# Split weights at rotating offsets inside their slots, in a one-layer decoder kernel

## The chip, the core and the metric

The kernel runs on one core of a Trainium2 chip. A core has a matrix engine, TensorE (PE in the profile; its weight loads have a row of their own, PEld), a vector engine (DVE), an engine for activation functions (ACT), a general one (POOL) and a queue that mostly issues transfers (SP). All but the last work on a memory of 128 partitions on the core; in this text a "column" is one 4-byte element of each partition. Matmul results go to a separate accumulation memory of eight banks. The metric is the device time of one execution in microseconds; lower is better. The time before is 1580.56 us, the median of three runs that went from 1579.78 to 1582.54 us.

## The reference

One layer of a hybrid decoder computes 256 prompt tokens and 8 single-token samples, 264 token columns in all, with a model width of 2048:

```
xn = rmsnorm(x, g_mix);  z = xn @ w_in
x  = x + concat(rglru_group(z), mlstm_group(z)) @ w_out
xq = rmsnorm(x, g_xa) @ w_xa_q
x  = x + cross_attention(xq, memory K/V) @ w_xa_o      # 4 heads of 512, 256 memory tokens
xf = rmsnorm(x, g_ffn)
x  = x + (silu(xf @ w_ffn_gate) * (xf @ w_ffn_up)) @ w_ffn_down   # inner width 5632
y  = rmsnorm(x, g_final)
```

For the prompt, the memory's keys and values are also projected from 256 memory tokens (`mem @ w_xa_k`, `mem @ w_xa_v`); for the samples they come from a cache. States of the recurrent groups, keys and values are outputs as well. All is 32-bit floating point, and nearly all of the arithmetic is in the products with the weights.

## The kernel before

Activations lie transposed: the model width on the partitions, tokens along the columns. A product with weights is cut into steps (the list `steps`); a step has one weight piece of 128 partitions by up to 2048 columns (1 MB), which yields 128 output rows for all 264 tokens. `load_piece` (line 142) brings piece i into one of three `raw` buffers from the SP queue, some steps ahead.

To keep 32-bit accuracy with fast matmuls, each operand is held as a high and a low part of a reduced-precision 32-bit type. `split_half` (line 150) does that for the weights, 1024 columns at a time: ACT writes the high part `wh`, a rounded copy of the raw piece, and DVE writes the low part `wl`, the raw piece minus `wh`. Each goes to one of four slots of its own (tags "wh" and "wl"), in turn. The activations are split in the same way by other helpers into tiles of tag "B", of which there are 26 slots; one such tile usually holds four chunks of 264 columns.

`mm3` (line 175) then multiplies with three matmuls per chunk of 128 columns of weights:

```
pe.matmul(ps, ah, bh, start=start, stop=False)
pe.matmul(ps, ah, bl, start=False, stop=False)
pe.matmul(ps, al, bh, start=False, stop=stop)
```

The first argument after `ps` is the operand that is loaded into the array, the second the one that streams. In the normal steps (`proj`), the loaded operand is a chunk of `wh`, `wh` again, then `wl`, and the streamed ones are chunk c of the activation's high part, of its low part, and of its high part again. A full step has 16 chunks and 48 matmuls. In the value projection (`pe_v`) the roles are swapped: the activation is loaded and 512 columns of `wh` or `wl` stream. The matmuls of the key projection stream 256 columns, those of the other steps 264.

The main loop at the end goes through the steps in order. It issues the load of a later piece, the evaluation of the step before's result, the splits of the next step's piece (`split_half(i + LS, 0)` and `(…, 1)`, at high priority), the step's matmuls, and then as much side work (gates, recurrences, attention for the samples on DVE and ACT) as an estimate of the engines' clocks allows. The order on each engine is settled by a scheduler that simulates the program's timeline; only SP's order is written out by hand.

The profile puts almost all instructions on line 60, the helper that records them, so its rows are told apart by tiles: `mm<-B,wh` is a matmul into an accumulation bank `mm`, streaming a B tile against a high part.

Of the kernel before, what the change touches and what calls it, by code (L numbers as in the profile page):

```python
# [11 lines left out]
F32R = mybir.dt.float32r  # L12
# [5 lines left out]
P = 128  # L18
# [62 lines left out]
def layer_kernel(ctx: ExitStack, tc, xT, memT, vec, wrg, w_in, w_out, w_q, w_k, w_v, w_o,  # L81
# [7 lines left out]
    sb = ctx.enter_context(tc.tile_pool(name="sb", bufs=1))  # L89
# [6 lines left out]
    def nm(s):  # L96
        uid[0] += 1
        return f"{s}_{uid[0]}"
# [51 lines left out]
    def split_half(i, h, parts=1):  # L150
        if i >= len(steps):
            return
        cols = steps[i][1]
        lo, hi = h * 1024, min(cols, (h + 1) * 1024)
        wh = sb.tile([P, 1024], F32R, tag="wh", bufs=4, name=nm("wh"))
        wl = sb.tile([P, 1024], F32R, tag="wl", bufs=4, name=nm("wl"))
        r = raws[i]
        n = (hi - lo) // parts
        with tc.high_priority():
            for o in range(0, hi - lo, n):  # L160
                st["split"] = act.activation(wh[:, o: o + n], r[:, lo + o: lo + o + n], AF.Copy)
                dve.tensor_sub(wl[:, o: o + n], r[:, lo + o: lo + o + n], wh[:, o: o + n])
        splits[i, h] = (wh, wl)
# [1027 lines left out]
    with tc.high_priority():  # L1191
        for c in range(KC):
            split(*xn(c), xres[:, c, :], V("g_mix", c))
            if c == 1:
                split_half(0, 0, 4)
            elif c == 3:
                split_half(0, 1, 2)

    pend = []
    for i, (src, cols, pef, evf, need) in enumerate(steps):  # L1200
# [12 lines left out]
        now = pe.clock  # L1213
        dve.clock, act.clock = max(dve.clock, now), max(act.clock, now)
        split_half(i + LS, 0)
        if i + LS < len(steps) and steps[i + LS][1] > 1024:
            split_half(i + LS, 1)
# [128 lines left out]
```

## Time and profile before

| | |
|---|---|
| median of three runs | 1580.56 us |
| the profiled execution's span, first to last instruction | 1577.6 us |
| TensorE matmuls, busy | 1560.9 us (99%), 12,356 |
| TensorE weight loads, busy | 1536.0 us (97%), 12,356 |
| DVE, busy | 1047.3 us (66%) |
| ACT, busy | 779.2 us (49%) |
| mean granted TensorE clock | 0.994 of full speed |
| from HBM to the core and back | 205 GB/s over the span |

A row of the groups reads: line, engine, operation, output from inputs, shape, count, then busy time in us, the mean duration of one in ns, and the idle time of the engine just before them with what ended it. Matmuls overlap in the pipeline, so the duration of one (285 ns) is far longer than the interval between two starts. In the table by stretches, a cell such as "100.00 (x827)" is the engine's busy time in the stretch and the number of its instructions that start there; PEclk is the granted clock, 1.00 being full speed. In the order of time, a row gives the start and the length in us of a run of like instructions and, after "x", how many there are.

### The profile page before, as it was taken

Reading aid. Unit: us, or ns where it says so; the run is one execution under the profiler, and the core shown is the slowest. Engines: PE = TensorE matmul, PEld = TensorE weight load, DVE = VectorE, ACT = ScalarE, POOL = GpSimd, SP = SyncE. Lnnn points to the kernel's source line nnn. Section 1 sums busy time; section 2 is a strip of 40 time slices with the busy share of each in tenths; the row PEclk is TensorE's granted clock in tenths of the full one; section 3 lists DMA queues with packets and bytes.
Section 4 is the critical chain, followed back from the end, with each engine's and each line's share of the span. In section 5 each row is a group of like instructions: output and inputs, shape, how many; then the busy total and the mean of one; then the engine's idle time right before and its main releaser. Section 6 shows DMA issues by size and latency. Waiting matters only on the chain.

```text
span 1577.6 us, 29752 instructions
## 1 busy us (share of the span) xinstructions
PE 1560.9 (99%) x12356; PEld 1536.0 (97%) x12356; DVE 1047.3 (66%) x2019; ACT 779.2 (49%) x1217; POOL 74.9 (5%) x142
## 2 busy tenths in 40 slices
PE   9999999999999999999999999999999999999997
PEld 9999999999999889989999999999999999999997
DVE  7976878787689999856655555455555554555554
ACT  7465775564445555545444444333444433344463
POOL 0001210001012112000000000000000000000000
PEclk9999999999999999999999999999999999999999
DMA  8445875547689888554545555455445555555452
GB/s 311 154 174 171 303 262 202 189 159 260 247 298 353 314 330 302 178 182 180 187 163 185 188 181 173 182 187 186 174 178 185 188 181 174 180 188 188 153 180 97
DMA packets 55303, 325.97 MB, mean 207 GB/s; under 512 B 6688, under 2 KB 7120, under 8 KB 24448
## 3 DMA queue, kind: packets, MB, share of 16 engines
q1 hardware_dynamic: 39744, 270.68, 47.9%
q0 software_dynamic: 15136, 53.16, 9.2%
q8 instruction: 96, 1.57, 0.4%
q10 hardware_dynamic: 288, 0.23, 0.1%
q14 instruction: 39, 0.32, 0.1%
HBM read 312.78 MB, written 11.28 MB: 205 GB/s over the span
## 4 chain that ended last, share of the span: by engine, by line
PE 97%; ACT 1%; DVE 1%; DMA 0%; issue 0%; SPq 0%; DVEq 0%; ACTq 0%
PE mm L60 92%; PE ax L60 6%; DVE B L60 1%; ACT B L60 1%; DMA xres<-xT 0%; ACT wh L60 0%; ACT L60 0%; DVE wl L60 0%; DVE c L60 0%; DVEq L1323 0%; DVE xres L60 0%; ACT t L60 0%; SPq L1185 0%; ACT rstd L60 0%; SPq L1178 0%
## 5 line engine op out<-in xcount | busy, mean ns | idle before, releaser
L60 PE MATMUL mm<-B,wh 128*128 128x264 f32 (+1 forms) x7520 | 1380.0, 285 | 2.8 <-DVE B L60 2.8
L60 PEld LDWEIGHTS mm<-B,wh 128*128 128x128 f32 x7520 | 1166.8, 189 | 4.4 <-ACT cso L60 2.9
L60 PE MATMUL mm<-B,wl 128*128 128x264 f32 (+1 forms) x3760 | 1066.9, 284 | 1.2 <-DVE wl L60 1.2
L60 ACT ACTIVATE wh<-raw 128x1024 fp32r<-128x1024 f32 (+2 forms) x518 | 538.4, 1041 | 710.1 <-PE mm L60 584.1
L60 DVE TENSOR_TENSOR wl<-raw,wh 128x1024 fp32r<-128x1024 f32 (+2 forms) x518 | 620.7, 1200 | 370.0 <-ACT wh L60 361.8
L60 PEld LDWEIGHTS mm<-B,wl 128*128 128x128 f32 x3760 | 708.8, 189 | 1.6 <-DVE wl L60 1.4
L60 DVE TENSOR_TENSOR t<-mm,rstd 128x264 f32<-128x264 f32 x104 | 44.9, 432 | 57.5 <-PE mm L60 57.5
L60 PE MATMUL mm<-wh,B 128*128 128x512 f32 x256 | 83.0, 398 | 0.0
L60 DVE TENSOR_TENSOR xres<-xres,mm 128x264 f32<-128x264 f32 x80 | 34.3, 428 | 46.5 <-PE mm L60 46.5
L60 PEld LDWEIGHTS mm<-wh,B 128*128 128x128 f32 x256 | 48.4, 189 | 10.5
L60 DVE SCALAR_TENSOR_TENSOR dw<-B,dw 128x256 f32<-128x256 f32 x128 | 53.8, 420 | 3.2 <-ACT dw L60 2.2
L60 PE MATMUL mm<-wl,B 128*128 128x512 f32 x128 | 51.0, 398 | 0.0
L60 PE MATMUL ax<-B,B 128*128 128x256 f32 (+3 forms) x288 | 48.7, 312 | 0.0
L60 DVE SCALAR_TENSOR_TENSOR dw<-B,qsm,dw 128x256 f32<-128x256 f32 x96 | 45.9, 480 | 1.2 <-ACT dw L60 0.6
L60 PEld LDWEIGHTS ax<-B,B 128*128 128x128 f32 x288 | 40.7, 189 | 3.4 <-issue 0.7
L1238 POOL TENSOR_TENSOR B<-B,rstd 128x264 f32<-128x264 f32 x4 | 2.8, 739 | 866.0 <-ACT rstd L60 866.0
L60 ACT ACTIVATE B<-xres,vecs 128x264 fp32r<-128x264 f32 (+1 forms) x64 | 31.2, 504 | 2.5 <-DMA xres<-xT 1.3
L60 ACT ACTIVATE t<-xres 128x264 f32<-128x264 f32 x60 | 23.8, 416 | 15.3 <-DVE xres L60 15.3
L60 PEld LDWEIGHTS mm<-wl,B 128*128 128x128 f32 x128 | 24.1, 188 | 5.1
L936 POOL DMA_DIRECT2D B<-kcT x32 | 17.3, 541 | 209.9 <-DVE B L60 119.3
L60 DVE TENSOR_TENSOR acc_x<-acc_x,t 128x264 f32<-128x264 f32 x59 | 25.3, 428 | 0.8 <-ACT t L60 0.5
L60 DVE SCALAR_TENSOR_TENSOR B<-xres,vecs,B 128x264 fp32r<-128x264 f32 x48 | 22.7, 489 | 4.5 <-ACT B L60 4.5
(152 smaller groups left out, 701.3 us busy)
## 6 DMA issues: line engine op xcount, KB each, us to landing
raw<-w_gu SPq DMA_DIRECT2D x88, 1024.0 KB, 4.8
raw<-w_in SPq DMA_DIRECT2D x40, 1024.0 KB, 4.8
raw<-w_d SPq DMA_DIRECT2D x32, 1024.0 KB, 4.8
raw<-w_out SPq DMA_DIRECT2D x16, 1024.0 KB, 4.8
B<-kcT POOLq DMA_DIRECT2D x32, 512.0 KB, 7.0
raw<-w_q SPq DMA_DIRECT2D x16, 1024.0 KB, 6.6
B<-vcT POOLq DMA_DIRECT2D x32, 512.0 KB, 7.6
raw<-w_k SPq DMA_DIRECT2D x16, 1024.0 KB, 7.2
```

The lines of the kernel that those rows point to most:

```text
L60: return f(*a, **k)
L936: pool_e.dma_start(kc, kcT[h, b])
L1238: e.tensor_mul(st["y"](c), st["y"](c), r)
```

## The change

The slots of `wh` and `wl` become 1136 columns wide, 112 more than a half piece needs, and a tile is the slice of 1024 columns that begins at an offset o in its slot. With k = 2i + h for half h of step i, o is 8 times (7k modulo 15) for the high part and 8 times (4k modulo 15) for the low part: fifteen offsets from 0 to 112 columns, 32 bytes apart, in one order for `wh` and in another for `wl`. Everything that reads or writes `wh` and `wl` uses the slice and is unchanged in the code.

```
         lo, hi = h * 1024, min(cols, (h + 1) * 1024)
-        wh = sb.tile([P, 1024], F32R, tag="wh", bufs=4, name=nm("wh"))
-        wl = sb.tile([P, 1024], F32R, tag="wl", bufs=4, name=nm("wl"))
+        k = 2 * i + h
+        wh, wl = (sb.tile([P, 1136], F32R, tag=t, bufs=4, name=nm(t))[:, o: o + 1024]
+                  for t, o in (("wh", 8 * (k * 7 % 15)), ("wl", 8 * (k * 4 % 15))))
         r = raws[i]
```

## The prediction

> **What bounds the kernel now.** Three parts of the page and three further views, in this order. First the busy shares and, of the part on the chain that ended last, the shares by engine.
>
> ```profile
> span 1577.6 us, 29752 instructions
> PE 1560.9 (99%) x12356; PEld 1536.0 (97%) x12356; DVE 1047.3 (66%) x2019; ACT 779.2 (49%) x1217; POOL 74.9 (5%) x142
> PE 97%; ACT 1%; DVE 1%; DMA 0%; issue 0%; SPq 0%; DVEq 0%; ACTq 0%
> ```
>
> TensorE (PE) holds 97% of the chain; DVE and ACT hold 1% each. So the time is the number of matmuls times the interval from one start to the next, plus little. A busy PE is not a PE at its peak, and the next views say how far from it. The groups of instructions, with different shapes kept apart, give the counts that the change touches: every matmul that has wh or wl as an operand.
>
> ```profile
> L60 PE MATMUL mm<-B,wh 128*128 128x264 f32 x7008 | 1286.5, 285 | 2.8 <-DVE B L60 2.8
> L60 PE MATMUL mm<-B,wl 128*128 128x264 f32 x3504 | 994.9, 284 | 1.2 <-DVE wl L60 1.2
> L60 PE MATMUL mm<-B,wh 128*128 128x256 f32 x512 | 93.5, 283 | 0.0
> L60 PE MATMUL mm<-wh,B 128*128 128x512 f32 x256 | 83.0, 398 | 0.0
> L60 PE MATMUL mm<-B,wl 128*128 128x256 f32 x256 | 72.0, 281 | 0.0
> L60 PE MATMUL mm<-wl,B 128*128 128x512 f32 x128 | 51.0, 398 | 0.0
> L60 PE MATMUL ax<-B,wh 128*128 128x264 f32 x64 | 13.5, 308 | 1.9 <-ACT wh L60 1.4 <-ACT B L60 0.3
> L60 PE MATMUL ax<-B,wl 128*128 128x264 f32 x32 | 9.4, 304 | 0.0
> ```
>
> These are 7008 + 3504 + 64 + 32 = 10,608 matmuls of 264 columns, 768 of 256 and 384 of 512: 11,760 of the 12,356. The idle times behind the bars are 5.9 us in all, so no wait on the conversions is worth speaking of. The 285 ns of one matmul overlaps with its neighbours; the interval comes from the table by stretches.
>
> ```profile
> core 0: us, PE busy (x) PEld busy (x) DVE busy (x) ACT busy (x) POOL busy (x), PEclk, DMA share, GB/s
> 8.00:10.00 2.00, 2.00 (x9) 2.00 (x10) 1.96 (x5) 1.59 (x4) 0.00 (x0) 0.50 1.08 447
> ...
> 800.00:900.00 100.00, 100.00 (x827) 100.00 (x827) 56.93 (x79) 43.25 (x54) 0.00 (x0) 1.00 0.50 177
> 900.00:1000.00 100.00, 100.00 (x827) 100.00 (x826) 55.69 (x69) 42.23 (x50) 0.00 (x0) 1.00 0.51 183
> 1000.00:1100.00 100.00, 100.00 (x826) 100.00 (x825) 51.13 (x55) 37.46 (x38) 0.00 (x0) 1.00 0.49 179
> 1100.00:1200.00 100.00, 100.00 (x827) 100.00 (x826) 55.89 (x69) 41.92 (x52) 0.00 (x0) 1.00 0.50 179
> 1200.00:1300.00 100.00, 100.00 (x828) 100.00 (x827) 53.97 (x64) 40.72 (x46) 0.00 (x0) 1.00 0.51 181
> 1300.00:1400.00 100.00, 100.00 (x828) 100.00 (x827) 52.29 (x58) 38.43 (x41) 0.00 (x0) 1.00 0.52 184
> 1400.00:1500.00 100.00, 100.00 (x827) 100.00 (x826) 55.85 (x71) 42.55 (x55) 0.00 (x0) 1.00 0.49 171
> ```
>
> With the full clock granted (1.00), 826 to 828 matmuls start in each 100 us: 120.8 to 121.1 ns each. The first row and the next fence, the order of time near the start, show the same 264-column matmul while the granted clock was 0.50.
>
> ```profile
> 9.42 0.64 PE L60 MATMUL ax<-B,wl 128*128 128x264 f32 x2
> 9.86 0.64 PE L60 MATMUL ax<-B,wh 128*128 128x264 f32 x2
> 10.30 0.42 PE L60 MATMUL ax<-B,wl 128*128 128x264 f32 x1
> 10.52 0.42 PE L60 MATMUL ax<-B,wh 128*128 128x264 f32 x1
> ```
>
> Two take 0.44 us, one 0.22 us. Twice the clock should make 110 ns of it; the table has 120.9. So 10.9 ns of each interval are not the streaming of columns at the granted clock: 10,608 x 10.9 ns = 116 us of the span. That loss is the only thing of weight that the place of an operand could change, and the forecast is a forecast of what it does.
>
> **The change part by part.** *Instructions.* Nothing is added, removed or moved: an offset is part of an operand's address. The same 11,760 matmuls, the same conversions, DMAs and order on every queue: 0 us. The wait for a free slot stays as it is (a ring of four slots each for high and low parts, handed over by PE), because a slice keeps the whole slot.
>
> *Slots of 1136 instead of 1024 columns.* Eight slots grow by 112 x 4 = 448 bytes each, 3,584 bytes of each partition. The tiles that lie behind them move; nothing is reloaded or made smaller: 0 us.
>
> *The conversions on ACT and DVE.* They write wh and wl at other places, and DVE reads wh there. The nearest rows are the same two operations on B tiles, which lie elsewhere:
>
> ```profile
> L60 DVE TENSOR_TENSOR wl<-raw,wh 128x1024 fp32r<-128x1024 f32 x496 | 606.9, 1225 | 369.2 <-ACT wh L60 361.0 <-PE mm L60 0.9
> L60 ACT ACTIVATE wh<-raw 128x1024 fp32r<-128x1024 f32 x496 | 525.7, 1061 | 700.0 <-PE mm L60 574.6 <-issue 105.9 <-ACT B L60 13.9
> L60 DVE TENSOR_TENSOR B<-B,B 128x1024 fp32r<-128x1024 f32 x4 | 4.9, 1222 | 0.5 <-ACT B L60 0.5
> L60 ACT ACTIVATE B<-B 128x1024 fp32r<-128x1024 f32 x4 | 4.2, 1055 | 0.4 <-PE ax L60 0.4
> ```
>
> 1222 against 1225 ns and 1055 against 1061 ns: by these rows the place is worth under 1% of a conversion, 6 ns. I take 0. What hides it: ACT waits 574.6 us for PE to free a slot and DVE 361.0 us for ACT, so both have time to spare. If that cover were gone, 496 x (3 + 6) ns = 4.5 us.
>
> *The matmuls.* This is the term that decides. By the code, in one weight tile of 1024 columns the weights of chunk c begin 512 bytes after those of chunk c-1, while the streamed operand of chunk c lies 1056 bytes after that of c-1 (264 columns of 4 bytes). So the distance between the two moves by 544 bytes from chunk to chunk, 17 steps of 32 bytes. The new offsets are multiples of 8 columns, 32 bytes: they shift the distances on the grid on which they already lie, and each step already runs through 16 of them. Different stages have different B tiles as streamed operand, hence other sets of distances, and the table's rows have the same interval for all of them within 0.3 ns. A second row speaks for that: the key projection streams 256 columns, so chunks are 1024 bytes apart and the distance moves by 512, never by an odd 32.
>
> ```profile
> 545.15 0.28 PE L60 MATMUL mm<-B,wl 128*128 128x256 f32 x1
> ...
> 546.57 0.28 PE L60 MATMUL mm<-B,wl 128*128 128x256 f32 x1
> ```
>
> Between these rows lie 12 matmuls: 1.42 us / 12 = 118.3 ns. Streaming is 110 x 256/264 = 106.7 ns, which leaves 11.6 ns against 10.9. Two quite different patterns of distances lose the same.
>
> What no row shows is a high and a low part at different offsets in their slots: now both begin at the start of slots of one size; after, the two starts differ by another multiple of 32 bytes at each tile. Bounds: if the whole loss went, the gain is 768 x 11.6 ns = 9 us on top of the 116 us, 125 us with the 512-column matmuls left as they are. If the place made every interval as long as the key projection's loss and the 264-column loss together, 22.5 ns, the cost is 11,760 x 11.6 = 136 us. I take 0, the value the seven equal rows are nearest to: an average over distances replaced by an average over other distances of the same grid.
>
> The Trainium skill, "SBUF — State Buffer", section "Who interferes with whom", says that PE never waits on anyone and gives it independent read ports for the streamed operand and the weights. By it the sum is 0 as well. The trace does not bear its strong form out, since 10.9 ns of each interval are left unexplained by streaming.
>
> *Sum.* 0 + 0 + 0 + 0 on the span of 1577.6 us. The median of the runs, 1580.56 us, is 2.96 us above that span, and I keep that difference: 1580.6 us. About 0.2%, 3.2 us, is what a measurement of this kernel can tell from no change; 3.2 us are 0.27 ns for each of the 11,760 matmuls.
>
> **The rivals.**
>
> *Slower on PE.* The load of a low part now falls elsewhere than that of the high part before it, and each such jump could lengthen the triple of matmuls around it (wh, wh, wl: 3504 + 256 + 128 + 32 = 3,920 triples). For it: triples do differ. In order of time, a steady stretch:
>
> ```profile
> 839.73 0.28 PE L60 MATMUL mm<-B,wl 128*128 128x264 f32 x1
> ...
> 840.08 0.28 PE L60 MATMUL mm<-B,wl 128*128 128x264 f32 x1
> ...
> 840.45 0.28 PE L60 MATMUL mm<-B,wl 128*128 128x264 f32 x1
> ...
> 840.81 0.28 PE L60 MATMUL mm<-B,wl 128*128 128x264 f32 x1
> ```
>
> 0.35, 0.37 and 0.36 us (rounded to 0.01): a span of up to 20 ns, within one step, with nothing changing but the place. Against it: seven stretches with the same mean. A sixth of the span, 3.3 ns for each triple, is 12.9 us: 1593.5 us. It decides from 0.8 ns per triple on.
>
> *Faster on PE.* The one offset of now is a poor one and the mean over fifteen is better. Same rows, same sixth: 1567.7 us. For it: a loss of 10.9 ns is there to be had. Against it: a step already runs through 16 distances.
>
> *Slower conversions.* At a start off a wider boundary, DVE could write or read more slowly and become the bound where it is fullest, the stage of the cached keys. The first row is all of it, the second its wl instructions alone:
>
> ```profile
> 500.00:650.00 150.00, 150.00 (x963) 136.37 (x962) 136.31 (x377) 87.35 (x170) 26.53 (x49) 1.00 0.82 308
> 500.00:650.00 150.00, 85.65 (x265) 49.78 (x265) 55.07 (x46) 1.00 0.82 308
> ```
>
> DVE has 150 - 136.31 = 13.7 us free beside 55.07 us of subtractions, so it decides from 25% on; at twice the duration 41 us are added: 1622 us. Against it stand 1222 and 1225 ns.
>
> *The loss goes.* Were the matmuls free of operand trouble at the new places, the intervals would fall to 110 ns plus a small fixed part. With a quarter of the loss left as that fixed part, 0.75 x 125 = 94 us are gone: 1487 us. The Trainium skill, "TensorE: Matmul & The Clock Gate", section "Wait — 56ns, not 53.3ns?", measured exactly that for back-to-back 16-bit matmuls: columns at the full clock and about 2.5 ns, here 112.5 ns. The trace has 120.9 ns, so by that rule something costs 8.4 ns of each interval that the page does not know; nothing in the rows says that it depends on the offset alone.
>
> That the change does nothing at all is not a case of its own: it gives the forecast's time.
>
> **How the numbers follow.** The forecast, within 0.2%: 0.54, with its own range 1577.4 to 1583.7 us (0.2% either way). Slower on PE 0.23, slower conversions 0.04: slower 0.27. Faster on PE 0.17, the loss goes 0.02: faster 0.19. Slower is put above faster because what the rows lack is the jump between high and low part, which can add a disturbance where now there is none. The range goes from 1567 to 1594 us, just past the times of the two near rivals: it leaves out the two far cases (0.06) and what of the near ones is larger than the sixth of the span (about a third of 0.40, 0.13), 0.19 together.
>
> **What would show it.** Right: 826 to 828 matmuls in each 100 us from 800 to 1500 us, wh at 1061 ns and wl at 1225 ns, the same 12,356 matmuls. Wrong on PE: 820 or fewer, or 834 or more, in those rows, with ACT's and DVE's durations unchanged. Wrong on the conversions: over 1500 ns for a subtraction, and waits of PE for wl. A different order of instructions, or a tile that no longer fits beside the larger slots, would break the first term.

## The result, and the profile after

The changed kernel is slower by a little: a median of 1585.77 us (1582.91 to 1587.89 us) against 1580.56 us (1579.17 to 1582.54 us) for the kernel before, 11 runs of each. The ratio is 1.0032 with a 95% interval of 1.0024 to 1.0040, so 0.32% or about 5.2 us.

The first parts of the page of the changed kernel, busy shares and shares of the chain that ended last:

```profile
span 1584.0 us, 29752 instructions
PE 1566.8 (99%) x12356; PEld 1541.6 (97%) x12356; DVE 1047.3 (66%) x2019; ACT 778.7 (49%) x1217; POOL 74.6 (5%) x142
PE 97%; ACT 1%; DVE 1%; DMA 0%; issue 0%; SPq 0%; DVEq 0%; ACTq 0%
```

The program is the same in kind and number: 29,752 instructions and 12,356 matmuls on both sides, and DVE's busy time agrees to 0.1 us. What grew is PE: 1566.8 - 1560.9 = 5.9 us of the span's 6.4 us. PE's idle time is the span less the busy time, 17.2 us against 16.7 us; so at most 0.5 us went to waits. The groups of instructions of the changed kernel, shapes apart, for the matmuls and conversions that the change touches:

```profile
L60 PE MATMUL mm<-B,wh 128*128 128x264 f32 x7008 | 1291.5, 286 | 2.8 <-DVE B L60 2.8
L60 PE MATMUL mm<-B,wl 128*128 128x264 f32 x3504 | 998.0, 285 | 1.1 <-DVE wl L60 1.1
L60 DVE TENSOR_TENSOR wl<-raw,wh 128x1024 fp32r<-128x1024 f32 x496 | 607.0, 1225 | 368.9 <-ACT wh L60 361.6
L60 ACT ACTIVATE wh<-raw 128x1024 fp32r<-128x1024 f32 x496 | 525.3, 1060 | 703.1 <-PE mm L60 580.3 <-issue 103.1 <-ACT B L60 13.8
```

The two conversions take 1060 and 1225 ns, as before (1061 and 1225 ns). The idle time behind the bars of the two matmul groups is 3.9 us, against 4.0 us. So neither a conversion nor a wait carries the 6 us. The table by stretches of the changed kernel does; its columns are the stretch, its length, then busy time and number of instructions on PE, weight loads, DVE, ACT and POOL, then the granted clock, the DMA share and GB/s:

```profile
800.00:900.00 100.00, 100.00 (x823) 100.00 (x822) 56.95 (x79) 43.08 (x53) 0.00 (x0) 1.00 0.51 179
900.00:1000.00 100.00, 100.00 (x822) 100.00 (x821) 55.26 (x67) 41.27 (x50) 0.00 (x0) 1.00 0.51 180
1000.00:1100.00 100.00, 100.00 (x823) 100.00 (x823) 49.75 (x53) 37.66 (x38) 0.00 (x0) 1.00 0.51 180
1100.00:1200.00 100.00, 100.00 (x821) 100.00 (x820) 56.02 (x69) 42.15 (x52) 0.00 (x0) 1.00 0.51 180
1200.00:1300.00 100.00, 100.00 (x823) 100.00 (x822) 54.36 (x64) 40.14 (x46) 0.00 (x0) 1.00 0.52 182
1300.00:1400.00 100.00, 100.00 (x825) 100.00 (x823) 51.91 (x58) 38.09 (x40) 0.00 (x0) 1.00 0.52 182
1400.00:1500.00 100.00, 100.00 (x822) 100.00 (x821) 54.73 (x67) 41.39 (x51) 0.00 (x0) 1.00 0.49 173
```

Each row has 821 to 825 matmuls where the kernel before had 826 to 828, at the same granted clock of 1.00. PE is never idle in these rows; each matmul starts a little later after the one before it. The same view cut into two long stretches, PE alone (stretch, length, busy time and number of matmuls, granted clock, DMA share, GB/s), first of the kernel before, then of the changed kernel:

```profile
800.00:1500.00 700.00, 700.00 (x5776) 1.00 0.51 179
0.00:700.00 700.00, 693.01 (x5202) 0.99 0.67 245
```

```profile
800.00:1500.00 700.00, 700.00 (x5746) 1.00 0.51 179
0.00:700.00 700.00, 692.49 (x5181) 0.99 0.68 245
```

From 800 to 1500 us the interval is 700 us / 5776 = 121.19 ns before and 700 us / 5746 = 121.82 ns after, 0.63 ns or 0.52% more. In these two stretches together 30 + 21 matmuls are missing; at 121 ns each that is 6.2 us, nearly all of the span's 6.4 us. The long row also corrects a small thing in the text above: a row counts the matmuls that overlap it, and not only those that start in it (the seven rows of the kernel before add up to 5790, the long row has 5776). So rows of 100 us give 120.9 ns where the long row gives 121.2.

### The profile page after: what moved, and what is told of

It reads as the page before. It is cut to its first block, busy times and chain, and to the rows that moved or that the text cites. A ratio compares the mean times of both kernels' runs of the same rounds, so it can differ in the third digit from the quotient of the medians.

```text
span 1584.0 us, 29752 instructions
## 1 busy us (share of the span) xinstructions
PE 1566.8 (99%) x12356; PEld 1541.6 (97%) x12356; DVE 1047.3 (66%) x2019; ACT 778.7 (49%) x1217; POOL 74.6 (5%) x142
## 4 chain that ended last, share of the span: by engine, by line
PE 97%; ACT 1%; DVE 1%; DMA 0%; issue 0%; SPq 0%; DVEq 0%; ACTq 0%
PE mm L60 92%; PE ax L60 6%; DVE B L60 1%; ACT B L60 1%; DMA xres<-xT 0%; ACT wh L60 0%; ACT L60 0%; DVE wl L60 0%; DVE c L60 0%; DVEq L1324 0%; DVE xres L60 0%; ACT t L60 0%; SPq L1186 0%; ACT rstd L60 0%; SPq L1179 0%
## 5 line engine op out<-in xcount | busy, mean ns | idle before, releaser
L937 POOL DMA_DIRECT2D B<-kcT x32 | 17.2, 539 | 213.7 <-DVE B L60 122.8
```

Source lines behind the costliest of these rows:

```text
L937: pool_e.dma_start(kc, kcT[h, b])
```

## The experiments

All but three of the experiments change only the two lines of `split_half` that allocate `wh` and `wl`: the width of a slot, and the offset (in columns of 4 bytes) of the high and of the low part in it. The first diff shows the lines of the kernel before; in the later ones they are the same and only the new lines stand. Each ratio is against runs of the kernel before on the same chip, with its 95% interval in brackets.

Three questions were put, in this order. Is it the offset at all, the width of the slot, or the difference between high and low part? If it is the place: an operand's own place, its move from tile to tile, or its place relative to the B tiles that stream against it? And can the loss that is already in the kernel before be taken away by a better place?

Beside the times, one more measure is used: the mean time of a full step of 48 matmuls of 264 columns, from the starts of its matmuls in the trace, for the steps from about 690 us on that no side work interrupts. It resolves single nanoseconds, where the runs resolve about a microsecond and a half in 1580. It is 5818 ns in the kernel before and 5849 ns in the changed one, 30 ns more. A tile's place modulo 256 bytes is that of the address which the built program gives it.

**The slots alone, and slots of 1152 columns.** Both keep every tile at the start of its slot.

```
-        wh = sb.tile([P, 1024], F32R, tag="wh", bufs=4, name=nm("wh"))
-        wl = sb.tile([P, 1024], F32R, tag="wl", bufs=4, name=nm("wl"))
+        wh, wl = (sb.tile([P, 1136], F32R, tag=t, bufs=4, name=nm(t))[:, o: o + 1024]
+                  for t, o in (("wh", 0), ("wl", 0)))      # e1_wide; e2_wide512 has 1152
```

> Slots of 1136 columns as in the change, but every tile begins at column 0 of its slot, so that only the size of the slots is left of the change. A slot is then 4544 bytes, and the low part's slot lies four of them, 18,176 bytes, behind the high part's: 256 bytes off a multiple of 512, where before the two lay a multiple of 4096 apart. Theory A (a low part that does not begin at the same place, counted modulo 512 bytes, as its high part costs time): slower than before, about 822 to 824 matmuls per 100 us between 800 and 1500 us, 1584 to 1587 us. Theory B (changing the offset from tile to tile costs time): the offset here does not change, but the slot starts still step by 448 bytes modulo 512, so part of the loss, 1582 to 1586 us. Theory C (the offsets alone, slots innocent): as before, 827 matmuls per 100 us, 1580.6 us.

> Slots of 1152 columns, every tile at column 0. A slot is 4608 bytes, nine times 512, so all tiles begin at one place modulo 512 bytes, as before, and high and low part lie a multiple of 512 (and of 2048, not of 4096) apart. Theory A: as before, 826 to 828 matmuls per 100 us, 1580 to 1581 us. Theory B: as before as well. A theory that larger slots, or the tiles behind them that move, cost time by themselves: slower, 1584 us or more.

With 1136 columns the time is 1583.53 us, a ratio of 1.0023 (1.0012 to 1.0035): slower, with no offset at all. With 1152 columns it is 1580.27 us, 1.0005 (0.9994 to 1.0015). The long stretch, PE alone, of the slots of 1136 and then of those of 1152:

```profile
800.00:1500.00 700.00, 700.00 (x5757) 1.00 0.51 179
```

```profile
800.00:1500.00 700.00, 700.00 (x5776) 1.00 0.51 179
```

5757 matmuls against 5776, which is also the number of the kernel before; the mean step is 5841 and 5818 ns. A slot of 1136 columns is 4544 bytes, 17 x 256 + 192; one of 1152 is 4608 bytes, 18 x 256; one of 1024 is 4096 bytes, 16 x 256. So in slots of 1136 a tile's place modulo 256 bytes moves from slot to slot even with all offsets at 0, and in the other two it does not. The prediction's term "slots of 1136 columns: 0" is the first that fails.

**Offsets, high and low part alike, in slots that do not themselves move the place.**

```
+        wh, wl = (sb.tile([P, 1152], F32R, tag=t, bufs=4, name=nm(t))[:, o: o + 1024]
+                  for t, o in (("wh", 8 * (i % 16)), ("wl", 8 * (i % 16))))   # e3_together
```

> Slots of 1152 columns; high and low part of a step begin at the same one of 16 offsets (8 columns apart), another one at each step. The distance between high and low part stays a multiple of 512 bytes. Theory A: as before, within 0.1%: 826 to 828 matmuls per 100 us, 1579 to 1582 us, with single steps that differ by up to 0.4%. Theory B: slower, like the change, 822 to 824 matmuls per 100 us, 1584 to 1588 us.

1584.54 us, 1.0026 (1.0017 to 1.0036). High and low part never differ here, so the greater part of the change's 0.32% needs no difference between them. The first row below is the long stretch of this kernel; the others are nine successive steps, each at an offset 32 bytes further than the one before it (0, 32, ... 224, and 256 bytes), modulo 256 bytes. A row counts 50 because two matmuls overlap its edges.

```profile
800.00:1500.00 700.00, 700.00 (x5761) 1.00 0.50 179
837.99:843.80 5.81, 5.81 (x50) 1.00 0.50 188
843.80:849.64 5.84, 5.84 (x50) 1.00 0.50 178
849.64:855.52 5.88, 5.88 (x50) 1.00 0.52 180
855.52:861.35 5.83, 5.83 (x50) 1.00 0.51 181
861.35:867.16 5.81, 5.81 (x50) 1.00 0.50 179
867.16:872.99 5.83, 5.83 (x50) 1.00 0.49 176
872.99:878.86 5.87, 5.87 (x50) 1.00 0.53 186
878.86:884.68 5.82, 5.82 (x50) 1.00 0.51 182
884.68:890.50 5.82, 5.82 (x50) 1.00 0.51 180
```

In this stage, the gate and up projections, the step takes 5.81 us at offsets 0 and 128 bytes, 5.87 to 5.88 us at 64 and 192, and values between at the odd multiples of 32. In the starts of the matmuls, steps of this stage at offsets 256 bytes apart agree within 1 ns (5812 and 5813, 5841 and 5840, 5876 and 5876, 5833 and 5834). So the place counts, it is worth up to 1.1% of a step, and it repeats every 256 bytes. (The last row, 5.82 us, holds the rounding of its edges; by the starts it is one of the 5813.) Which offset is the slow one depends on the stage, whose B tiles lie in another order. In the second down projection the offsets of 160, 192, 224 and 0 bytes take:

```profile
1287.20:1293.05 5.85, 5.85 (x51) 1.00 0.53 190
1293.05:1298.93 5.88, 5.88 (x50) 1.00 0.51 180
1298.93:1304.75 5.82, 5.82 (x51) 1.00 0.48 179
1304.75:1310.56 5.81, 5.81 (x51) 1.00 0.51 173
```

Here 192 bytes is slow (5886 ns by the starts), and 64 bytes is not (5818 ns).

**The low part alone.**

```
+        wh, wl = (sb.tile([P, 1152], F32R, tag=t, bufs=4, name=nm(t))[:, o: o + 1024]
+                  for t, o in (("wh", 0), ("wl", 8 * (i % 16))))   # e4_low_only
```

> Slots of 1152 columns; the high part at column 0 always, the low part at one of 16 offsets, another one at each step. Theory A: slower, like the change, 822 to 824 matmuls per 100 us, 1584 to 1588 us, and the one step in 16 whose low part is at offset 0 goes as fast as before. Theory B: half of the change's loss, since only one of the two parts moves, 1582 to 1585 us, and the steps at offset 0 are no faster than the others.

1585.53 us, 1.0037 (1.0024 to 1.0051). The long stretch, and again nine successive steps; the first and the last have the low part at a multiple of 256 bytes, as the high part has it in all of them:

```profile
800.00:1500.00 700.00, 700.00 (x5753) 1.00 0.52 179
849.72:855.53 5.81, 5.81 (x50) 1.00 0.53 185
855.53:861.38 5.85, 5.85 (x51) 1.00 0.53 183
861.38:867.23 5.85, 5.85 (x51) 1.00 0.52 171
867.23:873.07 5.84, 5.84 (x51) 1.00 0.54 184
873.07:878.93 5.86, 5.86 (x51) 1.00 0.52 185
878.93:884.77 5.84, 5.84 (x50) 1.00 0.50 178
884.77:890.65 5.88, 5.88 (x51) 1.00 0.55 181
890.65:896.48 5.83, 5.83 (x50) 1.00 0.54 185
896.48:902.29 5.81, 5.81 (x50) 1.00 0.49 188
```

These steps are of the gate and up projections. When the two parts lie alike the step takes 5.81 us; at the seven other offsets it takes 5.83 to 5.88 us. At 128 bytes, where both parts moved together cost nothing, a low part moved alone costs some 50 ns (the fifth step, 5.86 us). So the low part's place counts too; the mean step is 5841 ns, 23 ns above the kernel before, though only one matmul in three loads a low part. It is no rule that unlike parts are slower: by the starts, in the output projection of the cross-attention a low part 160 bytes on takes 5809 ns and one that lies like the high part 5822 ns. Nor does this run separate the low part's distance to the high part from its distance to the streamed tile; both change together.

**Everything moved.** A tile of 16 columns (64 bytes) that nothing reads is placed ahead of all others, so that weights and B tiles alike begin 64 bytes further on.

```
+    pad = const.tile([P, 16], F32, name="pad")        # e5_all_moved
+    nc.gpsimd.memset(pad, 0.0)
```

> The kernel before with an unused tile of 16 columns (64 bytes, cleared once on POOL) ahead of everything, so that raw pieces, B tiles, high and low parts all lie 64 bytes further on and keep every distance among them. Theory R (what counts is where the weights lie relative to the streamed operand, modulo 256 bytes): as before, 827 matmuls per 100 us, 1579 to 1581 us. Theory S (what counts is the weights' own place, whatever streams): slower, as the steps of the run with both parts moved together that had this place, 5.86 us for a step instead of 5.82, 821 matmuls per 100 us, 1589 to 1592 us.

**The weights alone moved, by the same 64 bytes, at every step alike.**

```
+        wh, wl = (sb.tile([P, 1152], F32R, tag=t, bufs=4, name=nm(t))[:, o: o + 1024]
+                  for t, o in (("wh", 16), ("wl", 16)))   # e6_place64
```

> Slots of 1152 columns, both parts always at column 16 of their slots, 64 bytes on from before; B tiles stay. In the run with both parts moved together the steps at this place took 5.86 us against 5.81 to 5.82 us at offset 0. Theories R and S alike: every step at 5.86 us, 819 to 821 matmuls per 100 us, about 0.7% slower: 1589 to 1592 us. A theory that it is the change of place from step to step that costs: as before, 1580 us.

These two are the pair that decides. With everything moved the time is 1580.63 us, 0.9997 (0.9986 to 1.0008), and the mean step is the 5818.3 ns of the kernel before. With the weights alone moved it is 1585.09 us, 1.0044 (1.0029 to 1.0059), and the mean step is 5854 ns. The long stretch, first with everything moved, then with the weights alone:

```profile
800.00:1500.00 700.00, 700.00 (x5778) 1.00 0.51 179
```

```profile
800.00:1500.00 700.00, 700.00 (x5741) 1.00 0.51 179
```

5778 against 5741 matmuls, with the weights at the same places modulo 256 bytes in both kernels. The wider slots of the second one are not the reason: with slots of 1152 columns and no offset the mean step was 5818 ns too. In fact the kernel before, that one and the one with everything moved agree to 1 ns in each stage: 5813 ns for a step of the cross-attention's output projection, 5820 in the gate and up projections, 5827 in the first down projection, 5807 in the second. So an operand's own place does not count; its place relative to what stayed does, and the next experiment ties that to the streamed B tiles. And a place that never changes from tile to tile can be slower than the change itself, so it is not the move that costs. The time came out below what was expected for this run: its stages differ, 5814 ns for a step in one and 5866 ns in another.

**B tiles all alike.** A B slot has 4224 bytes, 16.5 x 256, so in the kernel before the B tiles begin at one of two places modulo 256 bytes, 128 apart. One small B tile was made larger, which makes all 26 slots 4352 bytes, 17 x 256.

```
-    z = B([P, 2, 292])
+    z = B([P, 2, 544])                                # e7_even_b
```

> The kernel before with B slots of 4352 instead of 4224 bytes (one tile of that tag is made larger, its added columns unused), so that all B tiles, all high and all low parts begin at one place modulo 256 bytes; before, every second B slot lay 128 bytes off. Theory R: in the trace of before, groups of four chunks whose two streamed tiles both lie at the weights' place take 1447 ns, those with one of them 128 bytes off 1453 to 1459 ns, with both 1460 ns; if all become the first kind, a step takes 5.79 us instead of 5.82, 829 to 830 matmuls per 100 us, 1572 to 1575 us, faster than before by 0.4%. Theory S: as before, 1580 us.

1578.81 us, 0.9988 (0.9978 to 0.9997): faster by 0.12%, where 0.4% had been expected. It is the one version that beats both kernels. Its long stretches:

```profile
800.00:1500.00 700.00, 700.00 (x5783) 1.00 0.51 179
0.00:700.00 700.00, 693.55 (x5210) 1.00 0.68 245
```

7 and 8 matmuls more than in the kernel before. All the steps measured, in all stages, now take the same time, 5813.3 ns with a standard deviation of 0.9 ns (5.7 before): with the B tiles alike, the differences between the stages are gone. The expectation was read from groups of 12 matmuls (four chunks) in the kernel before. Over all the steps measured there, a group takes 1446 ns on average where streamed tiles and weights begin alike modulo 256 bytes, 1453 ns with the streamed high part 128 bytes off, 1462 ns with the streamed low part off, and 1460 ns with both off. But the groups of the first kind go from 1442 to 1453 ns, by their position in the step. In the new kernel all groups are of the first kind, and each takes 1453 ns. So the same distance does not always give the same time; what ran before a group is the likely reason, since the order of the groups is what differs.

One rival can be settled here: that PE is slowed by ACT, DVE or the DMA, which read and write the weight tiles and raw pieces meanwhile. The four rows are the four groups of one step, with only the instructions on raw pieces: busy time on DVE and on ACT (the conversions of the next step), granted clock, DMA share, GB/s.

```profile
904.48:905.93 1.45, 0.22 (x1) 1.06 (x1) 1.00 0.53 220
905.93:907.38 1.45, 1.01 (x1) 0.00 (x0) 1.00 0.00 0
907.38:908.84 1.46, 0.23 (x1) 1.06 (x1) 1.00 0.56 90
908.84:910.29 1.45, 0.99 (x1) 0.00 (x0) 1.00 0.96 407
```

ACT converts beside the first and third group only, DVE mostly beside the second and fourth, and the DMA share goes from 0.00 to 0.96, yet by the starts the four groups take 1453 to 1454 ns each.

The gain does not hold for every shape. By the starts (longer gaps left out), the 256-column matmuls of the key projection take 119.8 ns in this kernel against 117.9 before, and the 512-column ones of the value projection 227.5 against 231.8.

**The change's width, with high and low part in the same order.**

```
+        k = 2 * i + h
+        wh, wl = (sb.tile([P, 1136], F32R, tag=t, bufs=4, name=nm(t))[:, o: o + 1024]
+                  for t, o in (("wh", 8 * (k * 7 % 15)), ("wl", 8 * (k * 7 % 15))))   # e8_same_order
```

> The change with the high part's order of offsets used for both parts: only the other order for the low part is undone. High and low part then begin 256 bytes (modulo 512) apart in every tile, which by theory R, with a period of 256 bytes, is the same as no distance. Theory R: as the run with both parts moved together, half of the change's loss on PE: 824 matmuls per 100 us, 1583 to 1586 us. If the period were 512 bytes, as theory A of the first runs had it: no better than the change, 822 or fewer, 1586 us or more. If only the unlike places cost: as before, 827.

1584.04 us, 1.0024 (1.0014 to 1.0034), with a mean step of 5839 ns. Its long stretch:

```profile
800.00:1500.00 700.00, 700.00 (x5757) 1.00 0.51 179
```

5757 matmuls against the change's 5746. Since four slots of 4544 bytes are 71 x 256 bytes, high and low part lie alike here. By the step, about 20 of the change's 30 ns come with the moving place, and the last 10 ns with the other order of the low parts. In the times the interval of this run overlaps that of the change, so the split is carried by the steps and not by the times.

**Low part 192 bytes on, always.**

```
+        wh, wl = (sb.tile([P, 1152], F32R, tag=t, bufs=4, name=nm(t))[:, o: o + 1024]
+                  for t, o in (("wh", 0), ("wl", 48)))   # e9_low48
```

> Slots of 1152 columns, the high part always at column 0, the low part always at column 48 (192 bytes on). In the run with the low part alone moved, steps at that place took 5.86 us against 5.81 us with both at 0. Theory R (it is the place, not the move): all steps at 5.86 us, 819 to 821 matmuls per 100 us, 1589 to 1592 us. Theory B (what costs is that the low part moves from tile to tile): as before, 827 and 1580 us.

1587.73 us, 1.0053 (1.0035 to 1.0071), the slowest of all. The long stretch:

```profile
800.00:1500.00 700.00, 700.00 (x5720) 1.00 0.51 178
```

5720 matmuls are 0.97% fewer than before, and the mean step is 5874 ns, in the stage of gate and up projections 5892. No tile moves here. As with the weights moved by 64 bytes, the whole run lost less than expected, because other stages lose less.

**A shift of 16 bytes.**

```
+        wh, wl = (sb.tile([P, 1152], F32R, tag=t, bufs=4, name=nm(t))[:, o: o + 1024]
+                  for t, o in (("wh", 4), ("wl", 4)))   # e10_place16
```

> Slots of 1152 columns, both parts always at column 4, 16 bytes on, half of the smallest step of the change. If the place counts in units of 32 bytes and a start between two of them falls to the lower one: as before, 827 matmuls per 100 us, 1580 us. If it counts in finer units, or if a start off 32 bytes costs by itself: another value, between those of the places at 0 and at 32 bytes (827 and 824, 1580 to 1585 us) or below both.

1586.06 us, 1.0037 (1.0023 to 1.0050), with a mean step of 5853 ns. The long stretch:

```profile
800.00:1500.00 700.00, 700.00 (x5744) 1.00 0.51 179
```

So the grid of 32 bytes on which the prediction reasoned is not the finest on which places differ: half a grid step costs 34 ns of a step, as much as 64 bytes (36 ns).

**Chunks as far apart in the weights as in the activations.** Each chunk of 128 columns of weights begins 136 columns after the one before it, which is 544 bytes. That does not equal the 1056 bytes between streamed chunks, but it differs from them by 512 bytes, so within a tile the distance between the two stays constant modulo 256 bytes. Slots are 1088 columns, 4352 bytes, and the conversions write through a view with the gaps (`cv`); the value projection, where the weights stream, keeps them dense.

```
-                st["split"] = act.activation(wh[:, o: o + n], r[:, lo + o: lo + o + n], AF.Copy)
-                dve.tensor_sub(wl[:, o: o + n], r[:, lo + o: lo + o + n], wh[:, o: o + n])
+                x, y, z = r[:, lo + o: lo + o + n], wh[:, o: o + n], wl[:, o: o + n]
+                if apart:                                                    # e11_apart
+                    cs = slice(o // P, (o + n) // P)
+                    x, y, z = rv(x), cv(wh)[:, cs], cv(wl)[:, cs]
+                st["split"] = act.activation(y, x, AF.Copy)
+                dve.tensor_sub(z, x, y)
...
-            o = (c % per) * w
+            o = (c % per) * (136 if self.i not in vsteps else w)
```

> Chunks of weights begin 544 instead of 512 bytes apart (136 columns, of which 128 are used; slots of 1088 columns, the value projection's tiles left dense), so that the distance to the streamed operand moves by 512 bytes from chunk to chunk: it no longer runs through steps of 32 bytes, but stays at 0 or 128 bytes modulo 256 throughout. If the loss of 11 ns per matmul comes from the distances that a step runs through, and a constant good one has less: faster, 835 matmuls per 100 us or more, 1565 us or less. If a constant distance loses as much, as the key projection's 11.6 ns have it: 824 to 830 matmuls per 100 us, 1575 to 1586 us. ACT and DVE write in pieces of 128 columns here; if that makes them slower, their mean durations of 1061 and 1225 ns show it, with no effect on PE after 700 us.

1585.81 us, 1.0034 (1.0024 to 1.0044); the conversions keep their 1061 and 1224 ns. The long stretch:

```profile
800.00:1500.00 700.00, 700.00 (x5752) 1.00 0.51 179
```

5752 matmuls: 121.7 ns each. With a distance that does not change from chunk to chunk, the loss against streaming is still there, and even a little larger. So the 11 ns that a matmul loses on average are not the price of running through the distances, and no kernel tried here has more than 0.15 ns less of them (121.04 ns with the B tiles alike, 121.19 before). Where they come from stays open.

**What follows.** Four readings were in play in the expectations, there under letters: that places repeat with 512 bytes (A), that the move from tile to tile costs (B), that an operand's own place counts (S), and that the place relative to the streamed tile counts, modulo 256 bytes (R). The steps at equal places 256 bytes apart speak against the first; the fixed places of 64 and 192 bytes, as slow as or slower than any moving ones, against the second; the pair of everything moved and weights alone moved against the third. The fourth is left and no run contradicts it, but it needs two additions that it did not have: the distance alone does not fix the time, and what ran before probably counts (B tiles alike), and places differ on a grid finer than 32 bytes. By it, the kernel before happens to lie well. All its weights begin at 224 modulo 256 bytes and its B tiles at 224 or 96, so every group of four chunks starts from a distance of 0 or 128 bytes, with high and low part alike. The change replaces these by an average over many distances, most of them worse: with both parts moved together, six of the eight offsets modulo 256 bytes took longer in the gate and up projections than the 5820 ns of the kernel before. Why a relative place costs what it does was not shown.

## Why the prediction came out as it did

The forecast was 1580.6 us, within 0.2%. 1585.77 us lies inside the range of 1567 to 1594 us and 2 us outside the forecast's own range. What came is the side of the rival "slower on PE". That the time lies in the range is owed to the range being opened for that rival, and not to the reasoning behind the zero; that the real loss stayed under half of the rival's price is luck as far as the prediction goes, since no term of it gives that size.

*Instructions, 0 us: right.* The same 29,752 instructions, in the same order on each engine.

*Conversions, 0 us: right.* 1060 and 1225 ns, at offsets of all kinds; and at gaps between chunks as well, 1061 and 1224 ns. The comparison with the same operations on B tiles was a good one, because those tiles really lie elsewhere. "Slower conversions" falls with it.

*Slots of 1136 columns, 0 us: wrong.* The prediction counted bytes and asked what no longer fits. It did not ask what a slot's size does to the start of the next slot. By itself it costs 0.23% (0.12 to 0.35%), the offsets left out.

*Matmuls, 0 us: wrong, and this is the step that failed*: "an average over distances replaced by an average over other distances of the same grid". Measured, the term is 121.82 - 121.19 = 0.63 ns for each matmul from 800 to 1500 us, and 5.9 us of PE's busy time in all. Two faults lay under it.

The first: the seven rows were taken for seven samples of distances. They were seven looks at mixtures of the same few. Weights always began at 224 modulo 256 bytes and B tiles at 224 or 96, in every stage. Nor does a step run through 16 distances, as the prediction has it: a B tile holds four chunks and the next one begins anew, so modulo 256 bytes each group of four chunks runs through 0, 32, 64 and 96 bytes from a start at 0 or 128. The prediction looked at how distances move within a tile and not at where a tile starts, which the starts of the slots decide. Even so the rows were not quite equal, and the small difference was the sign. In the kernel before, the first down projection, the second one and the gate and up projections have, in 90 us each:

```profile
985.00:1075.00 90.00, 90.00 (x744) 1.00 0.50 186
1265.00:1355.00 90.00, 90.00 (x746) 1.00 0.53 186
1110.00:1200.00 90.00, 90.00 (x745) 1.00 0.49 177
```

These are the stages of 5827, 5807 and 5820 ns for a step, 0.34% from end to end. The prediction's row of 826 lies mostly in the first down projection, its rows of 828 partly in the second.

The second: the rows are too coarse for what they were to exclude. The bound that matters was 0.27 ns for a matmul. The key projection's 11.6 ns against 10.9 came from starts rounded to 0.01 us over 12 matmuls, 0.8 ns for each (over the whole key projection a matmul takes 117.9 ns, longer gaps left out, in both kernels: 11.2 ns above streaming), and a count of 827 in 100 us is good to 1 in 827, 0.15 ns, before the edges. A stretch of 700 us on both sides would have fixed the "before" to some 0.02 ns; but nothing in one trace could show a place that the kernel never had.

*The rival "slower on PE".* Its place was right (PE, with ACT and DVE unchanged), its price too high: 5.2 us against 12.9, or 1.3 ns for a triple against 3.3. Its threshold of 0.8 ns for a triple was passed. Its mechanism, a jump between high and low part, is not shown as such: a low part moved alone costs 23 ns for a step, but its distance to the streamed tile changes with it. In any case it is the smaller part of this change: high and low part moved alike already cost 16 to 23 ns of a step, against 30. The larger part is a mean over worse places, the very step that the forecast had put at zero.

*"Faster on PE"* rested on the one offset of now being a poor one. Of all the kernels tried it is nearly the best: the best, B tiles alike, is 0.12% faster. *"The loss goes"* falls with the chunks set apart and with every other run: no interval below 121.0 ns was measured in a full stretch (700 us / 5783).

The Trainium skill, "SBUF — State Buffer", section "Who interferes with whom", gives PE two independent read ports, for the streamed operand and for the weights, and names a port pair that PE does not use as the only cause of contention. Read literally, as the prediction read it, the place of an operand would cost nothing. The pair of runs with the weights at the same places modulo 256 bytes and the B tiles 64 bytes apart, 5778 and 5741 matmuls in 700 us, does not agree with that strong form: 0.64% hangs on the two operands' places.

*The marks set beforehand.* 826 to 828 in a row was to mean right, 820 or fewer wrong. The rows have 821 to 825, between the two. The marks were drawn from the rivals' prices, and the gap between them should have been divided at the 0.2% bound: 827 x 0.998 = 825.

## What to carry to other kernels

A change that only moves tiles is not free when matmuls bound the kernel: work out each operand's start modulo 256 bytes in every slot, before and after. Slot sizes that are multiples of 256 bytes keep streamed and loaded tiles at one place to each other, which makes the time steady; that the place is also a good one has to be measured, since a constant shift of 64 bytes cost 0.44% here. Before equal rows are used as evidence that something does not matter, ask whether it varied between them at all. Effects of tenths of a per cent are read from long steady stretches, by counts of matmuls at the same granted clock, and not from single starts.

## What the runs showed of the hardware that was not expected

The rate of matmuls with 32-bit reduced-precision operands depends on where the loaded operand begins relative to the streamed one: 5.81 to 5.89 us for one step of 48 matmuls of 264 columns within one kernel, by the offset of the weights and the B tiles of the stage, repeating every 256 bytes. Moving both operands together by 64 bytes changed nothing (5818.3 ns both times); moving one of them by 16 bytes cost 34 ns of a step.

The same relative place took 1442 to 1453 ns for 12 matmuls, by their position in the step, where groups at other places stood between, and 1453 ns where it was the only one. Yet within a stage of the kernel before each position in a step repeats within about 0.5 ns (standard deviation), so this is a fixed pattern and not noise.

On average 11 to 12 ns of each interval of 121.0 to 122.4 ns are left above the 110 ns of streaming in all thirteen kernels, whatever the places. No run here shows their cause.
